# A hybrid transformer block on one Trainium2 core: two late gate blocks as one product of seven, and block sums of the weights added on chip

## The chip, the core and the metric

The kernel runs on one core of one Trainium2 chip. Its engines work side by side, each through its own list of instructions in order, and wait for each other by semaphores. TensorE multiplies matrices: the profile calls it PE, and its weight loads PEld. VectorE (DVE) and ScalarE (ACT) do the elementwise work, GpSimd (POOL) issues transfers that add, and SyncE (SP) issues most other transfers. Matrix products end in PSUM, eight banks of 128 x 512 float32 values; everything else lies in SBUF (on chip) or in DRAM.

The metric is the time of one execution in microseconds (us), less is better. All matrices are float32 in DRAM.

## The reference

One layer with two mixers side by side and a feed-forward part, on 512 tokens of width 1024:

```python
def hybrid_layer(x, ...):
    xn = rmsnorm(x, n_mix_pre)
    proj = xn @ w_in
    qa, ka, va, za, beta_logit, a_dt, qb, kb, vb, gb, gate_a, gate_b = _split_cols(proj, IN_SIZES)
    qkv = jax.nn.silu(causal_depthwise_conv(jnp.concatenate([qa, ka, va], axis=-1), conv_a))
    ...
    oa = chunk_gated_delta_rule(qa, ka, va, beta, g)
    oa = rmsnorm(oa, norm_a) * jax.nn.silu(za.reshape(b, s, A_HEADS, A_DV))
    ya = oa.reshape(b, s, A_V) @ w_br_a
    ...
    ob = chunk_retention(qb, kb, vb)
    ob = rmsnorm(ob, norm_b.reshape(B_HEADS, B_DV)) * jax.nn.silu(gb.reshape(b, s, B_HEADS, B_DV))
    yb = ob.reshape(b, s, B_V) @ w_br_b
    mix = (jax.nn.sigmoid(gate_a) * ya + jax.nn.sigmoid(gate_b) * yb) @ w_out
    x = x + rmsnorm(mix, n_mix_post)
    hn = rmsnorm(x, n_mlp_pre)
    ff = jnp.square(jax.nn.relu(hn @ w_up)) @ w_down
    return x + rmsnorm(ff, n_mlp_post)
```

The columns of `w_in` that matter here: `za` (2048 columns, four blocks of 512, the gates of the delta rule), `vb` and `gb` (2048 each, values and gates of the retention, four heads of 512), `gate_a` and `gate_b` (1024 each).

## The kernel before

**Products in three passes.** To keep float32 accuracy, each operand is split into a high part and a remainder (`split_weights`, L138): ScalarE casts the raw weight tile to `whi` (L145), VectorE subtracts to get `wlo` (L146). Each product is three matmuls, high x high, high x low, low x high. A raw weight tile is 128 x 1024, 512 KB, loaded by the SP queue (L102 or L185). `whi` and `wlo` have three buffers each, the raw tiles two, and four once a second pool (`ych`) has been appended in the second phase.

**Seven products for eight.** Where 512 tokens meet 1024 columns, the product is cut into 2 x 2 x 2 blocks of 256 tokens, 512 rows of the weight and 512 columns. `seven` (L233) computes it with seven block products (Winograd's form of Strassen's method) where eight would be needed. For that it takes sums of blocks of x, made once on chip (`feature_sums`, L1265, called after the second recurrence), and sums of blocks of the weight (`BlockSums`, L152). A block product is two half products (ks = 0 and 1), each of one weight tile and 12 matmuls; its results, two tiles of 128 tokens x 512 columns, lie in a pair of PSUM banks. The products are named by their block of x: "11", "12", "22" and the sums "s1" to "s4". `out(th, ch, ...)` takes a finished block of the output, token half th and column half ch.

**The trickle.** The weight sums are made in DRAM. The SP queue copies a block (`copy_block`, L165), and the GpSimd queue adds another block to it by a transfer that adds (`add_block`, L132). Each unit has four sums, 8 copies and 8 adds of 512 KB. `pace` (L112) issues them behind the weight loads, as far as a budget of model time allows; `JOBS_FROM` is the model time from which it starts.

**Phase one, the delta rule.** The order of TensorE's work is written out by a planner (`Clock`, L618) that keeps a model time, with chains (the inverse, four recurrences, the gating) and fillers, products that it puts between their steps. The fillers stand in a list, each with the events that it needs:

```python
                (ya_filler(1), ("og1",)),
                (value_filler(3), ("og1",)),
                (query_filler(3), ("og1",)),
                (gate_filler(2), ("gate1",)),
                (ya_filler(2), ("og2",)),
                (gate_filler(3), ("gate2",)),
```

`gate_filler(g2)` (L1147) multiplies all tokens by one column block of `za` (4 token tiles x 8 k tiles x 3 passes) and puts Silu of it into `zz`, which has one buffer; the event `gate1` says that the gating of group 1 has used it. On the chip, the third gate group ran from about 312 to 341 us, the fourth from 435 to 467. `recurrence(g2)` (L1157) has four steps; a step multiplies by `kf`, `rt` (L1184), `kd` (L1194) and `dall` (L1213), with small VectorE and ScalarE work between. `gate_chain` (L1233) then gates, transposes and splits the result into `og` (L1258). Matmuls of the planner are pinned to their order; those of the second phase that follow, such as the query and key projections of `scores` (L1384), are not and are put in by a scheduler where it sees room.

**Phase two.** `ya_partial(3)` (L882), then the unit of `gate_a`, four heads each with scores, a value-and-gate unit (`values_and_gates`, L1355) and outputs, then the unit of `gate_b` (`gate_unit`, L1459; `gate_b`, L1504), the final loop (L1521 on) and `w_out`. Inside a unit, the matmuls are pinned to the order of the program (L281). `tc.high_priority(n)` lets an instruction go ahead of others that stand up to n later in the program.

## Time and profile before

| | us |
|---|---|
| median of 3 runs | 1349.88 |
| lowest and highest of them | 1347.24, 1351.58 |
| the profiled execution | 1347.26 |
| its span, first to last instruction | 1345.1 |
| TensorE busy in it | 1327.4 |
| VectorE busy in it | 884.8 |

Times inside the execution count from the start of the span. Matmuls overlap in the pipeline, so the mean duration of one (about 390 ns) is longer than the time from one start to the next; the price of a matmul is read from the chain of waits, which gives the time by which each piece moves the end. Names of tiles stand as output<-inputs, and for a matmul the moving operand comes first: `mm<-whi,actT` streams a weight tile against tokens, `mm<-actT,whi` streams tokens against a weight.

### The profile page before, as it was taken

Reading aid. Unit: us, or ns where it says so; the run is one execution under the profiler, and the core shown is the slowest. Engines: PE = TensorE matmul, PEld = TensorE weight load, DVE = VectorE, ACT = ScalarE, POOL = GpSimd, SP = SyncE. Lnnn points to the kernel's source line nnn. Section 1 sums busy time; section 2 is a strip of 40 time slices with the busy share of each in tenths; the row PEclk is TensorE's granted clock in tenths of the full one; section 3 lists DMA queues with packets and bytes.
Section 4 is the critical chain, followed back from the end, with each engine's and each line's share of the span. In section 5 each row is a group of like instructions: output and inputs, shape, how many; then the busy total and the mean of one; then the engine's idle time right before and its main releaser. Section 6 shows DMA issues by size and latency. Waiting matters only on the chain.

```text
span 1345.1 us, 17540 instructions
## 1 busy us (share of the span) xinstructions
PE 1327.4 (99%) x6639; PEld 1101.2 (82%) x6639; DVE 884.8 (66%) x1515; ACT 634.4 (47%) x1118; POOL 90.9 (7%) x99
## 2 busy tenths in 40 slices
PE   9999999999999999999999999999999999999997
PEld 7888778888888877888888888888889888888886
DVE  6889867475476357777467576679684745828535
ACT  5783426553343424553443443455265746346441
POOL 2201110011101010001001000000100000000000
PEclk9999999999999999999999999999999999999999
DMA  6339987489779685899499695565814543535421
GB/s 193 128 95 244 230 191 149 101 227 207 170 187 210 166 227 161 262 309 221 139 278 194 172 258 142 166 206 173 265 67 147 162 146 110 188 98 179 131 78 63
DMA packets 114691, 236.78 MB, mean 176 GB/s; under 512 B 7398, under 2 KB 31120, under 8 KB 114096
## 3 DMA queue, kind: packets, MB, share of 16 engines
q1 hardware_dynamic: 95792, 185.10, 43.6%
q0 software_dynamic: 16496, 43.69, 19.8%
q10 hardware_dynamic: 2320, 6.89, 1.4%
q8 instruction: 52, 0.85, 0.3%
q14 instruction: 31, 0.25, 0.1%
HBM read 231.43 MB, written 79.71 MB: 231 GB/s over the span
## 4 chain that ended last, share of the span: by engine, by line
PE 86%; DVE 6%; ACT 4%; DMA 3%; issue 1%; DVEq 0%; ACTq 0%
PE mm L627 16%; PE mm L276 13%; PE dl L276 12%; PE mm L92 11%; PE mm L93 11%; PE mm L94 11%; PE dl L627 6%; DMA raw<-in_w_in_dram 2%; DVE wlo L146 1%; PE tr L356 1%; PE dl L93 1%; PE dl L94 1%; PE dl L92 1%; PE tr L636 1%; PE mm L591 1%
## 5 line engine op out<-in xcount | busy, mean ns | idle before, releaser
L146 DVE TENSOR_TENSOR wlo<-raw,whi 128x1024 fp32r<-128x1024 f32 x253 | 309.0, 1224 | 243.8 <-ACT whi L145 243.2
L145 ACT CAST whi<-raw 128x1024 fp32r<-128x1024 f32 x253 | 265.9, 1052 | 403.0 <-PE mm L93 100.1
L627 PE MATMUL mm<-actT,whi 128*128 128x512 f32 x448 | 144.3, 403 | 0.0
L276 PE MATMUL mm<-whi,xsum 128*128 128x512 f32 x384 | 121.9, 390 | 0.0
L94 PE MATMUL mm<-hn,wlo 128*128 128x512 f32 (+1 forms) x288 | 105.4, 366 | 0.0
L93 PE MATMUL mm<-hn,whi 128*128 128x512 f32 (+1 forms) x288 | 105.3, 366 | 0.0
L92 PE MATMUL mm<-hn,whi 128*128 128x512 f32 (+1 forms) x288 | 105.3, 366 | 0.0
L627 PEld LDWEIGHTS mm<-actT,whi 128*128 128x128 f32 x448 | 80.6, 188 | 15.1
L276 PE MATMUL dl<-whi,actT 128*128 128x512 f32 x288 | 91.9, 389 | 0.0
L627 PE MATMUL mm<-whi,actT 128*128 128x512 f32 x256 | 87.8, 406 | 1.1 <-DVE qf L857 1.0
L627 PE MATMUL mm<-actT,wlo 128*128 128x512 f32 x224 | 87.8, 392 | 0.0
L276 PEld LDWEIGHTS mm<-whi,xsum 128*128 128x128 f32 x384 | 72.0, 188 | 14.7
L276 PE MATMUL mm<-wlo,xsum 128*128 128x512 f32 x192 | 74.8, 390 | 0.0
L627 PE MATMUL mm<-whi,og 128*128 128x512 f32 x192 | 64.3, 402 | 0.0
L276 PEld LDWEIGHTS dl<-whi,actT 128*128 128x128 f32 x288 | 54.1, 188 | 11.2
L94 PEld LDWEIGHTS mm<-hn,wlo 128*128 128x128 f32 x288 | 54.3, 189 | 8.8
L93 PEld LDWEIGHTS mm<-hn,whi 128*128 128x128 f32 x288 | 54.3, 189 | 8.7
L92 PEld LDWEIGHTS mm<-hn,whi 128*128 128x128 f32 x288 | 54.3, 189 | 8.7
L276 PE MATMUL dl<-whi,ffq 128*128 128x512 f32 x192 | 61.1, 389 | 0.0
L132 POOL DMA_DIRECT2D sums<-sums x36 | 29.9, 830 | 443.2 <-DMA sums<-in_w_in_dram 238.7
L627 PEld LDWEIGHTS mm<-whi,actT 128*128 128x128 f32 x256 | 48.1, 188 | 11.5 <-issue 1.7
L276 PE MATMUL dl<-wlo,actT 128*128 128x512 f32 x144 | 56.0, 389 | 0.0
(372 smaller groups left out, 2789.7 us busy)
## 6 DMA issues: line engine op xcount, KB each, us to landing
raw<-in_w_in_dram SPq DMA_DIRECT2D x97, 512.0 KB, 5.5
raw<-sums SPq DMA_DIRECT2D x72, 512.0 KB, 4.1
sums<-in_w_in_dram SPq DMA_DIRECT2D x48, 512.0 KB, 8.0
sums<-sums POOLq DMA_DIRECT2D x36, 512.0 KB, 7.9
raw<-in_w_up_dram SPq DMA_DIRECT2D x36, 512.0 KB, 4.2
raw<-in_w_down_dram SPq DMA_DIRECT2D x26, 512.0 KB, 3.8
sums<-in_w_in_dram POOLq DMA_DIRECT2D x24, 512.0 KB, 10.8
sums<-in_w_down_dram SPq DMA_DIRECT2D x24, 512.0 KB, 6.9
```

The costliest lines, as they stand in the source:

```text
L92: nc.tensor.matmul(ps, lh, rh, start=first, stop=False)
L93: nc.tensor.matmul(ps, lh, rl, start=False, stop=False)
L94: nc.tensor.matmul(ps, ll, rh, start=False, stop=last)
L132: tc.keep_in_program_order(nc.gpsimd.dma_start(dst, src, accum_op=ALU.add))
L145: nc.scalar.copy(hi[:, :n], raw[:, :n])
L146: nc.vector.tensor_tensor(lo[:, :n], raw[:, :n], hi[:, :n], ALU.subtract)
L276: m = nc.tensor.matmul(pss[t], lhs[i // 2], rhs[i % 2], start=first and k + i == 0, stop=k + i == 5, skip_group_check=not first,)
L356: nc.tensor.transpose(ps, src, ident)
L591: pin(nc.tensor.matmul(first_keys[f][:, 256:512], ws[w][:, kk, :], xs[x][:, 2 * j + kk, 256:512], start=False, stop=kk == 1 and i == 2, sk ...
L627: m = tc.keep_in_program_order(nc.tensor.matmul(*args, **kwargs))
L636: tc.keep_in_program_order(nc.tensor.transpose(ps, src, ident if by is None else by))
```

## The change

Four things change, and some smaller ones.

The gates of groups 2 and 3 become one filler, `late_gates_filler`, a product of seven over the two column blocks. It stands in the list where the third gate group stood and needs `gate1`; the fourth place is gone. `z_sums` holds its four weight sums, the first in the trickle. The results of group 3 lie in two tiles of their own (`Rows2`), for which `kd` keeps three of four chunks for each head.

The six units of phase two keep two of their four weight sums in DRAM (`full=False`). The other two are made on chip: the raw tile y of sum 3 gets the raw tile x of block 11 added in place after both have been split, and the raw tile of block 21 then gets y added. The order of products becomes 11, s3, s2, 12, 22, s1, s4.

`JOBS_FROM` goes from 60 to 150, and an add may be issued once all copies of its unit have been.

In the last unit the gating of token tiles 0 and 1 moves from `gate_b` into the final loop.

```diff
-JOBS_FROM, LOAD_US, COPY_US, ADD_US, BACKLOG = 60.0, 2.0, 2.0, 3.4, 6.0
+JOBS_FROM, LOAD_US, COPY_US, ADD_US, BACKLOG = 150.0, 2.0, 2.0, 3.4, 6.0
...
+            self.made = (2, 1, 3, 0) if full else (2, 0)
...
+        def raw(self, i, ks):
             while any(job[0] is self for job in trickle):
                 copy_block()
-            while any(dst is t for dst, src in later_adds for t in self.parts):
+            while any(dst is t for dst, *_ in later_adds for t in self.parts):
                 add_block()
-            return block_weights(self.t[i - 1][:, 2 * ks : 2 * ks + 2, :])
+            return block_raw(self.t[i - 1][:, 2 * ks : 2 * ks + 2, :])
...
+    z_sums = BlockSums(w_in, OFF_ZA + 1024, OFF_ZA + 1536, "z")
+    ga_sums = BlockSums(w_in, OFF_GA, OFF_GA + 512, "ga", False)
+    vg_sums = [BlockSums(w_in, OFF_VB + h * 512, OFF_GB + h * 512, f"vg{h}", False) for h in range(4)]
+    gb_sums = BlockSums(w_in, OFF_GBR, OFF_GBR + 512, "gb", False)
...
+        def plus(dst, raws):
+            with tc.high_priority(SUM_PRIO):
+                for d, r in zip(dst, raws):
+                    nc.vector.tensor_tensor(d, r, d, ALU.add)
...
+        x, y = raws(sums.first_raw, 1), raws(sums.raw, 3)
         a = bank(psx)
-        plain(a, "11", 0, c1, True)
+        times(a, "11", x, True)
         with tc.high_priority(400):
             for t in range(2):
                 nc.scalar.copy(p1[t], a[t])
         b = bank(psm)
-        summed(b, "s2", 2, True)
+        times(b, "s3", y, True)
+        plus(y, x)
         with tc.high_priority(400):
             for t in range(2):
-                nc.vector.tensor_tensor(u2[t], p1[t], b[t], ALU.add)
+                nc.vector.tensor_tensor(u3[t], p1[t], b[t], ALU.add)
+        x = raws(sums.first_raw, 3)
         c = bank(psm)
+        times(c, "s2", y, True)
         with tc.high_priority(400):
             for t in range(2):
+                nc.vector.tensor_tensor(p1[t], p1[t], c[t], ALU.add)
+                nc.vector.tensor_tensor(u3[t], u3[t], c[t], ALU.add)
+        times(a, "12", x, False)
+        out(0, 0, a)
+        plus(x, y)
+        d = bank(psm)
+        times(d, "22", x, True)
+        out(1, 0, d, u3, ALU.add)
+        c = bank(psm)
+        times(c, "s1", raws(sums.raw, 1), True)
+        out(1, 1, c, u3, ALU.subtract)
+        times(c, "s4", raws(sums.first_raw, 2), False)
+        out(0, 1, c, p1, ALU.subtract)
...
+        def late_gates_filler():
+            z2 = zzs[2] = pa2.tile([P, 4, T], F32, tag="zz", name="zz")
+            parts = pa2.tile([P, 2, T], F32, name="zz3"), pa2.tile([P, 2, T], F32, tag="qf", name="zz3", bufs=3)
+            zzs[3] = Rows2(parts)
...
+            yield from product(a, "11", None, True)
...
+            yield from product(b, "s2", 2, True)
...
+            yield from product(a, "12", None, False)
+            silu(0, 0, a)
+            yield from product(b, "s3", 3, False)
...
+            yield from product(c, "s1", 1, True)
...
+            yield from product(d, "22", 4, True)
...
+            clock.done("z2", 2.0)
+            yield from product(c, "s4", None, False, OFF_ZA + 1536)
...
+            clock.done("z3", 2.0)
...
-                (gate_filler(2), ("gate1",)),
+                (late_gates_filler, ("gate1",)),
                 (ya_filler(2), ("og2",)),
-                (gate_filler(3), ("gate2",)),
...
-                        nc.vector.tensor_tensor(u[t], ps[t], u[t], op)
-                        out1(row, u[t])
+                        v = tmp("v_s")
+                        nc.vector.tensor_tensor(v, ps[t], u[t], op)
+                        out1(row, v)
...
-                nc.vector.tensor_tensor(sc[:, :n2], ps[:, n - n2 : n], dec[:, :n2], ALU.mult)
+                with tc.high_priority(400):
+                    nc.vector.tensor_tensor(sc[:, :n2], ps[:, n - n2 : n], dec[:, :n2], ALU.mult)
...
             nc.scalar.activation(tb, src, AF.Tanh, scale=0.5)
+            if t < 2:
+                return
...
-                    nc.vector.scalar_tensor_tensor(m, m, 1.0, pss[i][half], ALU.add, ALU.mult)
-                    nc.vector.tensor_tensor(m, m, acc_rows(t, half), ALU.add)
+                    total = pss[i][half]
+                    if t < 2:
+                        rest, total = ya[t // 2][:, t % 2, hs], acc_rows(t, half)
+                        nc.vector.tensor_tensor(total, total, pss[i][half], ALU.add)
+                    else:
+                        rest = acc_rows(t, half)
+                    nc.vector.scalar_tensor_tensor(m, m, 1.0, total, ALU.add, ALU.mult)
+                    nc.vector.tensor_tensor(m, m, rest, ALU.add)
```

## The prediction

> **What bounds the kernel now.** I read the page first: busy times, granted clock, the chain that ended last.

> ```profile
> span 1345.1 us, 17540 instructions
> ...
> PE 1327.4 (99%) x6639; PEld 1101.2 (82%) x6639; DVE 884.8 (66%) x1515; ACT 634.4 (47%) x1118; POOL 90.9 (7%) x99
> ...
> PEclk9999999999999999999999999999999999999999
> ...
> PE 86%; DVE 6%; ACT 4%; DMA 3%; issue 1%; DVEq 0%; ACTq 0%
> ```

> TensorE is busy for 1327.4 of 1345.1 us at full clock and is 86% of the chain. The time is the number of its matmuls plus the few places where it waits. Second, the matmul engine's waits over the whole run, the three longest:

> ```profile
> PE tr L636 <- DVE og L1258: 1.5, 2, 1.2
> PE dl L93 <- DVE wlo L146: 1.4, 1, 1.4
> ...
> PE dl L627 <- DVE rn L1021: 1.0, 1, 1.0
> ```

> No wait is long: what can be won is matmuls, and what can be lost is a new wait in an order that is now almost gapless. Third, the chain of waits inside the second value-and-gate unit (start, length, what):

> ```profile
> 656.49 5.44 PE dl L276 x24
> 661.93 5.44 PE mm L276 x24
> ...
> 672.81 10.88 PE mm L276 x48
> 683.69 5.44 PE dl L276 x24
> 689.13 5.44 PE mm L276 x24
> ```

> Seven products of 24 matmuls follow each other without a gap. One 128x512 matmul costs 5.44 / 24 = 0.227 us of TensorE's time; this is the price of the change's main term. Fourth, busy time by stretch (PE, PEld, DVE, ACT, POOL, clock, DMA share, GB/s): the third gate group, the query and key projections after the delta rule, the first gate unit, the value-and-gate unit above, the last gate unit.

> ```profile
> 312.30:340.60 28.30, 28.26 (x133) 23.40 (x132) 12.31 (x16) 10.78 (x19) 3.19 (x4) 1.00 0.90 193
> ...
> 467.40:496.00 28.60, 28.14 (x131) 22.38 (x130) 15.77 (x36) 10.42 (x23) 2.85 (x3) 1.00 0.73 163
> ...
> 523.90:562.20 38.30, 38.30 (x171) 31.72 (x170) 26.17 (x33) 18.90 (x24) 1.13 (x1) 1.00 0.72 212
> 656.50:694.60 38.10, 38.10 (x169) 31.55 (x169) 24.61 (x27) 19.58 (x23) 1.97 (x2) 1.00 0.81 239
> 889.60:930.10 40.50, 40.43 (x185) 32.69 (x185) 33.40 (x50) 22.66 (x30) 0.00 (x0) 1.00 0.64 202
> ```

> VectorE has 12 to 14 us free in the units, 7 in the last one.

> **Part 1, the late gates.** Column blocks 2 and 3 were two products of 4 token tiles x 8 k tiles x 3 passes, 192 matmuls. Seven products of 2 x 4 x 3 make 168. Removed: 24 x 0.227 = 5.44 us, all on TensorE's path. Added beside it: ten 128x512 VectorE additions and two ScalarE copies, with two weight splits fewer (14 for 16); VectorE is busy 12.3 of 28.3 us there, so they are hidden. The block sums of x are needed some 5 us after 312 instead of 529; the last of them starts at 288.1:

> ```profile
> L212 DVE TENSOR_TENSOR xsum<-full,xsum x4: 1219/1220/1221, 280.2 to 288.1; 128x1024 fp32r<-128x1024 f32 x4
> ```

> The weight sums of the late gates go first in the trickle: 8 copies and 8 adds. In the last 126 us before they are needed the old kernel already landed 12 copies and 14 adds:

> ```profile
> sums<-in_w_in_dram SPq DMA_DIRECT2D x12, 512.0 KB, 6.2
> ...
> sums<-sums POOLq DMA_DIRECT2D x7, 512.0 KB, 8.0
> sums<-in_w_in_dram POOLq DMA_DIRECT2D x7, 512.0 KB, 10.7
> ```

> So they are there in time; cost zero, hidden by the fillers ahead of them. Later units drop 24 copies and 24 adds, so 16 of each fewer in all, on the SP and POOL queues.

> **Part 2, the trickle starts later (60 to 150).** Its first copy left at 95.98, so it moves to about 186. In the stretch that it leaves, one weight load took 13.6 us, against 5.5 in the median, and the chain runs through it:

> ```profile
> 95.98 0.67 SPq L165 DMA_DIRECT2D sums<-in_w_in_dram  x1
> ```
> ```profile
> raw<-in_w_in_dram SPq DMA_DIRECT2D x97, 512.0 KB, 5.5
> ```
> ```profile
> 126.50 13.62 DMA raw<-in_w_in_dram
> ...
> 140.22 1.06 ACT whi L145
> ...
> 141.31 1.22 DVE wlo L146
> ...
> 142.93 2.24 DVE rn L1021
> ```
> ```profile
> 143.87 0.39 PE L627 MATMUL mm<-actT,wlo 128*128 128x512 f32 x1
> 145.31 1.07 PE L627 MATMUL dl<-rn,acc 32*32 32x32 f32 x32 [1.05 <-DVE rn L1021]
> ```

> VectorE works in order: behind the late split stands the end of the inverse, and TensorE stands 145.31 - 143.87 - 0.23 = 1.2 us for it. A load of the median length lets the split start some 2 us earlier, and the wait goes: -1.2 us (bounds: 0, if VectorE's order alone is late, to -1.2).

> **Part 3, the six second-phase units.** Each makes two sums in place, four VectorE additions of 128x1024. The nearest row is the same operation on SBUF tiles:

> ```profile
> L204 DVE TENSOR_TENSOR full<-actT x4: 1217/1218/1221, 226.3 to 273.0; 128x1024 f32<-128x1024 f32 x4
> ```

> 4 x 1.22 = 4.9 us, and two more 128x512 additions out of PSUM at 0.64 (the row at 683.24 below): 6.2 us. VectorE goes to 32.4 of 38.3 and 30.8 of 38.1 us; in the last unit eight operations of about that size leave it (5.1 us), so 34.5 of 40.5, and four return in the final loop. The whi ring has three buffers, so each split has two half products, 5.4 us, of lead; an addition of 1.2 us fits. Four raw buffers now hold x and y through two products, but a buffer is free again four half products (10.9 us) before its next tile is needed, against a load of 5.5. Throughput: zero.

> The order of products is new: "s4" accumulates onto bank pair c directly after "s1", while the subtraction out(1,1) must first read c. Before, "22" (5.44 us) lay between that read and "s4". The orders of matmuls are written out by hand, so everything behind waits with it. Price from the same kind of read behind product "s3":

> ```profile
> 682.10 1.23 DVE L146 TENSOR_TENSOR wlo<-raw,whi 128x1024 fp32r<-128x1024 f32 x1 [1.49 <-ACT whi L145]
> 683.24 1.28 DVE L254 TENSOR_TENSOR p<-p,mm 128x512 f32<-128x512 f32 x2
> ```

> The first read ends at about 683.24 + 0.64 = 683.88; the next product starts at 683.69. In the new order it would start 0.2 us late, with the signal 0.3. The second read has a further 1.36 us and is in time. Bounds for one unit: 0 (the split is issued behind the read) to 1.5 (one more split of 1.2 ahead of it). I take 0.3, since the splits fall in step with the half products: 6 x 0.3 = +1.8 us, bounds 0 and 9.

> [...]

> **Part 4, the tail of the delta rule.** Both late gates now run before the last recurrence. It began at 433.0 and ended at 472.8, with 96 matmuls of the last gate between its steps and the 96 of the next projections behind:

> ```profile
> 433.04 1.02 PE L627 MATMUL dl<-vt,rt 128*128 128x256 f32 x4
> ...
> 472.77 0.66 PE L627 MATMUL dl<-vn,dall 128*128 128x256 f32 x2
> ```
> ```profile
> L627 PE MATMUL mm<-whi,actT 128*128 128x512 f32 x64 | 22.1, 409 | 0.0
> L93 PE MATMUL mm<-actT,whi 128*128 128x512 f32 x32 | 13.3, 415 | 0.0
> ```
> ```profile
> 487.98 0.75 DVE L1258 SCALAR_TENSOR_TENSOR og<-tr,vecs,og 128x512 fp32r<-128x512 f32 x1 [1.47 <-ACT og L1256]
> 490.27 0.75 DVE L1258 SCALAR_TENSOR_TENSOR og<-tr,vecs,og 128x512 fp32r<-128x512 f32 x1 [1.54 <-ACT og L1256]
> ```

> All that stood between the late gates and it moves back by 72 matmuls, 16.3 us: it starts at 449.4. Its cover is the projections, 3 x 32 matmuls = 21.8 us, which are not pinned and can fall between its steps. Its own work is 39.7 - 96 x 0.227 = 17.9 us at most. A step with little filler took

> ```profile
> 216.42 1.03 PE L627 MATMUL dl<-vt,rt 128*128 128x256 f32 x4
> ...
> 222.14 1.13 PE L627 MATMUL dl<-vt,rt 128*128 128x256 f32 x4
> ```

> 5.7 us, so four take about 23. Projections done at 496.0 - 5.4 = 490.6; the gated features come 490.3 + 0.75 - 472.8 = 18 us after the recurrence, and two of the four, enough for the first 12 matmuls, 4.6 us earlier. 449.4 + R + 13.6 <= 490.6 gives R <= 27.6 us; at 23 nothing is lost. I take +0.6 for two or three short waits (bounds 0 and 12.1, R as long as before).

> **Sum**, against the profiled execution (1347.26 us, 2.2 around its span): -5.4 - 1.2 + 1.8 + 0.6 = -4.2, 1343.1. That execution was 2.6 below the median of the runs, 1349.88; on the median: **1345.7 us**, 0.31% less. This measurement can tell about 0.3%, 4 us, from no change: the forecast lies on that bound.

> **Rivals.** *No new waits*: the reads come ahead of the splits, and the 1.4 us wait at L93 for a late split goes with the lighter DMA. -5.4 - 1.2 - 1.4 = -8.0: 1341.9. For it: the free VectorE time above. Against: the split that ends just ahead of the read at 683.24. *The reads queue behind one more split or a value's rounding*: 1.4 per unit, 6 x 1.4 = 8.4; -5.4 - 1.2 + 8.4 + 0.6 = +2.4: 1352.3. At half of that price, -1.8: 1348.1. For it: the value units' out() has no priority of its own; against: the idle 1.49 us in front of each split. *The last recurrence stretches*, the one that ends slower: the list order puts projections between all its steps, R stays at the old 39.7, the gated features are 12.1 us late and nothing else is ready: -5.4 - 1.2 + 1.8 + 12.1 = +7.3: 1357.2. It costs time from R = 27.6 and makes the kernel slower than before from about R = 32.4. For it: R was 39.7 with 96 matmuls as cover; against: the 5.7 us step. *The early wait is VectorE's own*: +1.2, 1346.9, within the forecast's range.

> [...]

> **How the numbers follow.** Forecast (own range 1343.5 to 1348) 0.55, of which 0.30 falls under the bound of -4 us; no new waits 0.17, all faster; queued reads 0.16, a quarter slower; stretched recurrence 0.12, of which 0.10 slower. Faster 0.47, same 0.39, slower 0.14. The range 1341 to 1354 leaves out the stretched end and half of the best case's spread, about 0.2.

> **What would show it.** 24 fewer 128x512 matmuls in phase one; no wait for L1021; loads of the median length between 95 and 185; at the start of each s4 product a TensorE wait of 0.2 to 0.4 us for the subtraction, and none at the other products; the last recurrence starting near 448 and shorter than 28 us, with projections between its steps. Wrong would be waits over 1 us at s4, a gap before the fourth branch product, or waits for sums that have not landed.

## The result, and the profile after

The changed kernel took 1346.11 us in the median of 15 runs (1342.22 to 1349.96), the kernel before 1350.01 in 15 runs beside it (1346.46 to 1352.98). The ratio is 0.9965, with a 95% interval of 0.9953 to 0.9978. The forecast was 1345.7.

First the page and the waits of TensorE over the whole run, as they were read before (waits: us in total, times, longest):

```profile
span 1345.5 us, 17468 instructions
...
PE 1324.8 (98%) x6615; PEld 1096.7 (82%) x6615; DVE 930.4 (69%) x1563; ACT 638.3 (47%) x1126; POOL 78.3 (6%) x83
...
PE 83%; DVE 7%; ACT 4%; DMA 4%; issue 1%; DVEq 0%; ACTq 0%
```
```profile
PE tr L663 <- DVE og L1364: 2.7, 1, 2.7
PE dl L654 <- ACT vt L1314: 2.6, 1, 2.6
...
PE mm L303 <- DVE u L1574: 0.4, 1, 0.4
```

The records hold 24 matmuls fewer, and neither the wait for L1021 nor the one at L93 is there. Two waits of 2.6 and 2.7 us are new or longer, and the DMA's share of the chain rose from 3% to 4%. The span did not shrink with the median: the profiled execution took 1347.26 us, as that of before did. It is one of the slower of its 15 runs, that of before one of the faster of its own. A ledger of the stages shows where the gains go in these executions (time of the first or last matmul of a stage by the timeline; "again" is a second profiled execution of the changed kernel):

| | before | changed | again |
|---|---|---|---|
| first step of the first recurrence | 190.7 | 189.1 | 190.1 |
| first matmul of the late gates (before: of the third gate group) | 312.3 | 312.2 | 312.6 |
| first matmul of the first gate unit | 523.9 | 520.8 | 520.8 |
| last matmul of head 0's outputs | 606.7 | 604.5 | 604.4 |
| last matmul of head 3's outputs | 889.4 | 888.1 | 888.0 |
| last branch product of the final loop | 955.2 | 955.6 | 955.1 |
| last matmul | 1337.2 | 1337.6 | 1337.0 |

Phase one wins 3.1 us where the forecast had 6.0 (5.4 + 1.2 - 0.6), and wins none of it before the late gates begin (312.2 and 312.6 against 312.3). Then 0.9 is lost up to the outputs of head 0, 0.9 up to those of head 3, and 1.3 to 1.8 in the last unit and the final loop.

The chain of waits inside the late gates shows what was lost there (start, length, what):

```profile
334.02 1.05 ACT whi L145
335.10 1.24 DVE wlo L146
336.35 7.29 DMA raw<-sums
343.72 1.06 ACT whi L145
344.80 1.24 DVE wlo L146
346.05 6.73 DMA raw<-in_w_in_dram
...
352.89 1.04 ACT whi L145
353.93 0.75 ACT vt L1314 x2
...
354.72 2.63 PE dl L654 x8
```

In the kernel before, TensorE alone stood on the chain here. Now a loop stands on it: cast, subtract, and only then the load of the tile that takes the same buffer. There are two raw buffers, so one turn (9.7 us from 334.02 to 343.72) serves two tiles, 24 matmuls, 5.44 us of TensorE's work. A raw tile of the old gates served 24 matmuls by itself; one of a block product serves 12. When the cast at 352.89 comes late, the scaling of the recurrence (L1314) stands behind it on ScalarE, and TensorE waits 2.6 us for that. Behind this wait the clock is halved for 3.41 us, which costs 1.7 more (last section).

### The profile page after: what moved, and what is told of

The parts are those of the page before. It is cut to its first block, busy times and chain, and to the rows that moved or that the text cites. A ratio compares the mean times of both kernels' runs of the same rounds, so it can differ in the third digit from the quotient of the medians.

```text
span 1345.5 us, 17468 instructions
## 1 busy us (share of the span) xinstructions
PE 1324.8 (98%) x6615; PEld 1096.7 (82%) x6615; DVE 930.4 (69%) x1563; ACT 638.3 (47%) x1126; POOL 78.3 (6%) x83
## 3 DMA queue, kind: packets, MB, share of 16 engines
q1 hardware_dynamic: 88592, 167.27, 39.7%
## 4 chain that ended last, share of the span: by engine, by line
PE 83%; DVE 7%; ACT 4%; DMA 4%; issue 1%; DVEq 0%; ACTq 0%
PE mm L654 15%; PE mm L303 14%; PE mm L93 11%; PE mm L92 11%; PE mm L94 11%; PE dl L303 9%; PE dl L654 5%; DVE wlo L146 2%; DMA raw<-in_w_in_dram 2%; DMA raw<-sums 2%; PE dl L94 1%; PE dl L92 1%; PE dl L93 1%; PE tr L383 1%; PE tr L663 1%
## 5 line engine op out<-in xcount | busy, mean ns | idle before, releaser
L145 ACT CAST whi<-raw 128x1024 fp32r<-128x1024 f32 x259 | 272.1, 1052 | 415.3 <-PE mm L93 104.1
L146 DVE TENSOR_TENSOR wlo<-raw,whi 128x1024 fp32r<-128x1024 f32 x259 | 316.0, 1223 | 216.3 <-ACT whi L145 215.1
L654 PE MATMUL mm<-actT,whi 128*128 128x512 f32 x448 | 144.3, 403 | 0.0
L93 PE MATMUL mm<-hn,whi 128*128 128x512 f32 (+1 forms) x288 | 105.3, 366 | 0.0
L654 PE MATMUL mm<-actT,wlo 128*128 128x512 f32 x224 | 87.7, 392 | 0.0
L654 PE MATMUL mm<-whi,actT 128*128 128x512 f32 x176 | 61.3, 410 | 1.0 <-DVE qf L892 1.0
L93 PEld LDWEIGHTS mm<-hn,whi 128*128 128x128 f32 x288 | 54.3, 189 | 8.7
L303 PE MATMUL dl<-whi,actT 128*128 128x512 f32 x192 | 61.1, 389 | 0.0
L1771 DVE TENSOR_TENSOR ffq<-r,ffq 128x512 fp32r<-128x512 f32 (+2 forms) x51 | 33.8, 678 | 29.1 <-ACT ffq L1771 29.0
L92 PE MATMUL mm<-actT,whi 128*128 128x512 f32 x128 | 51.5, 403 | 0.0
L132 POOL DMA_DIRECT2D sums<-in_w_in_dram x28 | 32.6, 1167 | 321.3 <-DMA sums<-in_w_in_dram 321.0
L94 PE MATMUL mm<-actT,wlo 128*128 128x512 f32 x128 | 50.8, 397 | 0.0
## 6 DMA issues: line engine op xcount, KB each, us to landing
raw<-in_w_in_dram SPq DMA_DIRECT2D x95, 512.0 KB, 4.8
raw<-sums SPq DMA_DIRECT2D x56, 512.0 KB, 4.0
raw<-in_w_up_dram SPq DMA_DIRECT2D x36, 512.0 KB, 3.9
sums<-in_w_in_dram SPq DMA_DIRECT2D x32, 512.0 KB, 7.4
sums<-in_w_in_dram POOLq DMA_DIRECT2D x28, 512.0 KB, 8.1
raw<-in_w_down_dram SPq DMA_DIRECT2D x26, 512.0 KB, 3.8
sums<-in_w_down_dram SPq DMA_DIRECT2D x24, 512.0 KB, 12.5
sums<-sums POOLq DMA_DIRECT2D x16, 512.0 KB, 8.3
```

Source lines behind the costliest of these rows:

```text
L92: nc.tensor.matmul(ps, lh, rh, start=first, stop=False)
L93: nc.tensor.matmul(ps, lh, rl, start=False, stop=False)
L94: nc.tensor.matmul(ps, ll, rh, start=False, stop=last)
L132: tc.keep_in_program_order(nc.gpsimd.dma_start(dst, src, accum_op=ALU.add))
L145: nc.scalar.copy(hi[:, :n], raw[:, :n])
L146: nc.vector.tensor_tensor(lo[:, :n], raw[:, :n], hi[:, :n], ALU.subtract)
```

## The experiments

All ratios are to the kernel before, run beside each on the same chip.

**The change again**, unaltered.

> The changed kernel once more, unaltered, for a second profiled execution beside the first. Theory (late weights): each raw tile of the late gates serves 12 matmuls, 2.72 us, and with two raw buffers a tile takes half of a load and its split, (5.4 + 1.1 + 1.2) / 2 = 3.9 us, so TensorE waits there in every execution: 5 to 8 us lost between 300 and 375, in other places than the first time, and a median of 1346 +- 1. Rival (an accident of the one execution): under 3 us lost there, with no TensorE wait above 1.5 us in the late gates, and the same median.

1343.97 us (12 runs, 1342.19 to 1348.13; before 1350.74), ratio 0.9957 [0.9944, 0.9970]. Its profiled execution, of 1346.76 us, has the two waits at the same places; TensorE's waits:

```profile
PE dl L654 <- ACT vt L1314: 2.4, 1, 2.4
PE tr L663 <- DVE og L1364: 2.0, 1, 2.0
```

Late weights are no accident of one execution. The median of 1346 +- 1 that went with this theory was missed: it is 1 us lower.

**Two raw buffers more in the late gates.** The tile that later holds the values of group 3 takes every second weight tile.

```diff
+            def late(block):
+                if 3 not in vts and clock.events.get("og1", float("inf")) <= clock.now:
+                    vts[3] = pa2.tile([P, 4, 4, P], F32, tag="vt", name="vt", bufs=2)
+                n = next(seen) if 3 in vts else 0
+                if n % 2 == 0:
+                    return block_raw(block)
+                raw = vts[3].rearrange("p a c n -> p (a c n)")[:, 1024 * (n // 2 % 2) :][:, :1024]
```

> The changed kernel with two more raw buffers for the late gates, from the time on at which the first delta values are transposed: the tile that later takes the values of group 3 holds every second weight tile of the late gates. Theory (late weights, two buffers too few): a tile then takes 7.7 / 4 = 1.9 us, less than its 2.72 us of matmuls; the waits between 325 and 370 go, -3 to -5.5: 1341 to 1343, ratio 0.993 to 0.995. Rival (the DMA is full: 0.81 busy there): the loads only start earlier and take longer, -1 or less, ratio 0.996. Rival (VectorE's and ScalarE's order: splits ahead of the recurrence's scaling): the waits for the scaling stay or grow, 1346 or more.

1343.94 us (6 runs, 1341.86 to 1345.45), ratio 0.9960 [0.9945, 0.9976]. TensorE's waits between 303 and 375:

```profile
PE tr L663 <- DVE og L1379: 2.2, 1, 2.2
PE mm L654 <- DVE wlo L146: 0.8, 1, 0.8
PE mm L654 <- ACT whi L145: 0.5, 1, 0.5
```

The wait for the scaling is gone, and from 320.83 on the chain is TensorE's alone again, although each load took longer (median 7.7 to 9.4 us against 5.4 to 5.9). The first gate unit starts at 517.5, 6.4 earlier than before the change; the changed kernel won 3.1. The other traces say the same: the first gate unit starts at 517.3 to 518.5 in the three kernels with the two more buffers, and at 519.7 to 525.2 in the eight executions of kernels that have the late gates without them. So the mechanism is shown in profiled executions, where its price here is 3.3 us. The median did not follow: 1343.94 against 1343.97, which is what the rival of the full DMA expected. How large the loss is in the other runs stays open.

**Product s4 in a bank pair of its own**, with two VectorE operations more.

```diff
-        times(c, "s4", raws(sums.first_raw, 2), False)
-        out(0, 1, c, p1, ALU.subtract)
+        with tc.high_priority(400):
+            for t in range(2):
+                nc.vector.tensor_tensor(p1[t], c[t], p1[t], ALU.subtract)
+        e = bank(psx)
+        times(e, "s4", raws(sums.first_raw, 2), True)
+        out(0, 1, e, p1, ALU.add)
```

> The changed kernel, but product s4 of each of the six units starts in a bank pair of its own; the difference c - p1 is taken while it runs and s4 is added to it, two more 128x512 VectorE operations per unit. Theory (the read of s1 ahead of s4 costs 0.3 in a value unit, 0.9 in the first gate unit, up to 2 in the last): the waits for L1574 and its like at s4 go, -1.5 to -3 against the changed kernel: 1341 to 1343, ratio 0.993 to 0.9945. Rival (the two operations more only move the wait to the next product or the transposes): within 0.5 of the changed kernel, ratio 0.9955 to 0.997, with waits at the start of the scores or the last transposes in place of those at s4.

1342.84 us (6 runs, 1342.31 to 1344.76), ratio 0.9950 [0.9931, 0.9970]. The stretches by the ledger:

| us | before | changed | s4 in own banks |
|---|---|---|---|
| first gate unit to outputs of head 0 | 82.8 | 83.7 | 82.8 |
| from there to outputs of head 3 | 282.7 | 283.6 | 282.8 |
| from there to the last branch product | 65.8 | 67.6 (again 67.1) | 66.6 |

The first gate unit and the value units have their old length again, so the read of s1 ahead of s4 is their whole cost: 0.9 in the first row, which holds the value unit of head 0 too, and 3 x 0.3 in the second. In the last unit the read explains 0.5 to 1.0, and 0.8 is left. The medians do not tell this kernel from the changed one.

**22 between s1 and s4**, the order of products 11, s3, s2, 12, s1, 22, s4.

```diff
-        d = bank(psm)
-        times(d, "22", x, True)
-        out(1, 0, d, u3, ALU.add)
         c = bank(psm)
         times(c, "s1", raws(sums.raw, 1), True)
         out(1, 1, c, u3, ALU.subtract)
+        d = bank(psm)
+        times(d, "22", x, True)
+        out(1, 0, d, u3, ALU.add)
```

> The changed kernel with the order 11, s3, s2, 12, s1, 22, s4 in the six units: 5.44 us of product 22 lie again between the read of s1 and s4, with no operation more. Theory (the read costs): the same -1.5 to -3 as with banks of their own, ratio 0.993 to 0.9945. Rival (raw buffers): the summed tile of 22 is held through s1, so a load for s4 starts one product, 5.4 us, later; a load takes 4.4 to 4.9 us and its split 2.3, so TensorE waits for wlo at s4, 0.5 to 2 per unit: +1 to +9, ratio 0.997 to 1.003.

1354.65 us (12 runs), ratio 1.0035 [1.0021, 1.0050]: slower, in the direction of the rival. TensorE's waits between 525 and 800:

```profile
PE tr L383 <- DVE og L369: 3.0, 2, 1.8
PE mm L303 <- DVE wlo L146: 1.5, 2, 0.8
```

It waits for wlo as the rival said, but loses more where transposes wait for the split of the gated features, which neither side named. The order is not the only difference: an add of the trickle is issued at 548.8 in the first gate unit, where the changed kernel issues none between 528.4 and 570.9.

**The trickle from 60 again**, the rest as changed.

```diff
-JOBS_FROM, LOAD_US, COPY_US, ADD_US, BACKLOG = 150.0, 2.0, 2.0, 3.4, 6.0
+JOBS_FROM, LOAD_US, COPY_US, ADD_US, BACKLOG = 60.0, 2.0, 2.0, 3.4, 6.0
```

> The changed kernel with the trickle from 60 again. Theory (the forecast): the wait of 1.2 us for L1021 near 145 comes back, +1.2, 1345 to 1347, ratio 0.9965 to 0.9975. Rival (the trickle's adds cost where they fall on loads with little lead): adds that are done 90 us earlier leave the units freer, the late gates too: -1 to -4, ratio 0.993 to 0.995.

1357.56 us (6 runs, 1354.11 to 1360.44), ratio 1.0058 [1.0037, 1.0080]. Both expectations missed: by the ratios (1.0058 against 0.9965 and 0.9957) the early start costs 12.6 to 13.6 us, not 1.2. TensorE's waits:

```profile
PE mm L303 <- DVE u L1574: 7.1, 1, 7.1
...
PE dl L654 <- DVE rn L1056: 1.9, 1, 1.9
```

The wait of the forecast is back (the second line, the old L1021), and a far larger one stands in the first gate unit. The timeline there (start, busy, what, idle before and its releaser):

```profile
556.54 1.04 ACT L145 CAST whi<-raw 128x1024 fp32r<-128x1024 f32 x1 [4.34 <-DMA raw<-in_w_in_dram]
...
557.62 1.23 DVE L146 TENSOR_TENSOR wlo<-raw,whi 128x1024 fp32r<-128x1024 f32 x1 [4.01 <-ACT whi L145]
...
558.76 1.28 DVE L1574 TENSOR_TENSOR u<-mm,u 128x512 f32<-128x512 f32 x2
...
559.59 0.76 PE L303 MATMUL mm<-whi,xsum 128*128 128x512 f32 x1 [7.05 <-DVE u L1574]
```

A load is late, its split stands ahead of the read of s1 on VectorE, and s4 waits for the read: the forecast's rival of reads that queue behind a split, made worse by a late load. The loads and adds issued between 535 and 556, here and then in the changed kernel (KB each, median us to landing):

```profile
raw<-in_w_in_dram SPq DMA_DIRECT2D x4, 512.0 KB, 13.7
...
sums<-sums POOLq DMA_DIRECT2D x1, 512.0 KB, 8.3
sums<-in_w_down_dram POOLq DMA_DIRECT2D x1, 512.0 KB, 15.2
```
```profile
raw<-in_w_in_dram SPq DMA_DIRECT2D x4, 512.0 KB, 5.5
```

With two adds of the trickle beside them the same loads take 13.7 us; with none, 5.5.

**The trickle from 60 and s4 in its own banks**, the two edits above together.

> The changed kernel with the trickle from 60 and with product s4 in a bank pair of its own. Theory (the early trickle costs 10 us because its adds fall on the weight loads of the first gate unit, the last split is late, and the read of s1 stands behind it on VectorE, with s4 behind the read): without the read only the lateness of the split is left; the 7.1 us at 552 shrink to 1 or 2, the waits before the outputs stay away, and the 1.2 at L1021 remains: 1344 to 1348, ratio 0.996 to 0.999. Rival (the loads themselves are 7 us late, whatever waits for the read): 1352 or more, with waits for wlo in the first gate unit in place of L1574.

1353.79 us (12 runs), ratio 1.0035 [1.0018, 1.0051]. The wait of 7.1 us is gone; what is left of waits from 530 to 610 is small, the longest 0.9 us, though the loads still took 12.7 us. The largest in total:

```profile
PE dl L307 <- DVE wlo L146: 1.2, 2, 0.8
```

From the first gate unit's start to the outputs of head 0 it takes 87.7 us, against 94.1 with s4 in the old banks and 82.8 before the change, so the read did multiply the lateness there. But 1344 to 1348 was expected, and the median is 6 us above. In this execution TensorE also waits 3.3 us for the recurrence's scaling in the late gates, and the first gate unit starts at 525.2, 4.4 later than in the changed kernel. That part does not come with the early trickle in every execution: with the old banks the first gate unit started at 519.7, earlier than in the changed kernel.

**The late gates alone**: the six units as before, with four sums each in DRAM; the trickle from 150.

```diff
-    ga_sums = BlockSums(w_in, OFF_GA, OFF_GA + 512, "ga", False)
+    ga_sums = BlockSums(w_in, OFF_GA, OFF_GA + 512, "ga")
...
-        x, y = raws(sums.first_raw, 1), raws(sums.raw, 3)
+        plain, summed = block_products(src, sums, product)
```

> The late gates as a product of seven and the trickle from 150, with the six units, their four sums in DRAM and the last gating as before the change. Theory (late weights): -5.4 for 24 matmuls, -1.2 for the early wait, -1.4 for the wait at 510, +5 to +6.5 of new waits in the late gates: -1.5 to -3, 1347 to 1348.5, a ratio of 0.998 to 0.999. Rival (the forecast's sum: the late gates cost nothing at the side): -5.4 - 1.2 + 0.6 = -6.0, 1344, a ratio of 0.9955.

1360.32 us (6 runs, 1352.68 to 1365.12), ratio 1.0082 [1.0055, 1.0109]. Both missed. The profiled execution is the lowest of the six, 7.6 below their median, so it shows only a part of the loss. Up to the first gate unit it won 2.6, in the first unit of the down projection it lost 5.7, where adds and copies still ran (issues from 1040 to 1092, KB each, median us to landing; no copy and no add is issued there in the changed kernel):

```profile
raw<-in_w_up_dram SPq DMA_DIRECT2D x5, 512.0 KB, 12.7
...
sums<-in_w_down_dram SPq DMA_DIRECT2D x4, 512.0 KB, 11.8
sums<-in_w_down_dram POOLq DMA_DIRECT2D x4, 512.0 KB, 16.5
```

**The same with the trickle from 60.**

> The late gates as a product of seven, with the six units as before (four sums each in DRAM) and the trickle from 60. Theory (the trickle is too late: with 16 jobs more than before and a start at 150, the sums of the down projection are still being added when its first unit runs, which lost 5.8 us there): with the start at 60 this loss goes: 1345 to 1349, ratio 0.996 to 0.999. Rival (the volume: more adds beside the loads wherever they fall): 1353 or more, ratio 1.002 or more.

1353.46 us (12 runs), ratio 1.0033 [1.0013, 1.0052]. The start at 60 takes the loss in the down projection from 5.7 to some 1 us, as the theory said, but the time stays in the rival's range. Its execution loses 3.7 in the late gates at the state of the recurrence (the line below), and reaches the first gate unit at 524.1, no earlier than before the change; 4.0 more go up to the outputs of head 0. In this execution the volume costs as well, in other places.

```profile
PE dl L637 <- DVE st L1287: 3.7, 1, 3.7
```

**The units alone**: the gates of groups 2 and 3 as two products of all tokens.

```diff
-                (late_gates_filler, ("gate1",)),
+                (gate_filler(2), ("gate1",)),
                 (ya_filler(2), ("og2",)),
+                (gate_filler(3), ("gate2",)),
```

> The six units with two sums added in place, the trickle from 150 and the last gating as in the changed kernel; the gates of groups 2 and 3 are two products of all tokens again. Theory (late weights): the units cost 1.1 in the middle and 2.0 at the end, -1.2 to -1.6 early, -1.4 at 510: +0 to +1, 1350 to 1351, a ratio of 1.000 to 1.001. Rival (the units are the gain, the late gates give all of theirs back): -2 or more, ratio 0.9985 or less. Rival (the forecast's sum): -1.2 + 1.8 = +0.6, the same time as the theory; the waits at s4 then stand at 0.3 each.

1353.48 us (7 runs), ratio 1.0039 [1.0022, 1.0057]; every expectation was lower. Most of the loss is again in one place, TensorE's longest wait, with 1.7 us at a halved clock behind it:

```profile
PE mm L302 <- DVE u L1574: 3.3, 1, 3.3
```

With eight copies and adds fewer ahead of them, two adds of the down sums reach the first gate unit, and its four loads take 9.9 us.

**The kernel before with the trickle from 150.**

```diff
-JOBS_FROM, LOAD_US, COPY_US, ADD_US, BACKLOG = 60.0, 2.0, 2.0, 3.4, 6.0
+JOBS_FROM, LOAD_US, COPY_US, ADD_US, BACKLOG = 150.0, 2.0, 2.0, 3.4, 6.0
```

> The kernel before, with the trickle from 150 in place of 60 and nothing else. Theory (a late start pays only where the volume has shrunk): the wait for L1021 goes, -1.2, but 72 copies and adds start 90 us later, so that more of them fall on the units and on the first down projection: +2 to +8, 1352 to 1358, ratio 1.0015 to 1.006. Rival (the forecast's step by itself): -1.2 and no other difference, ratio 0.998 to 1.0.

1351.61 us (12 runs), ratio 1.0018 [1.0004, 1.0033]. The wait for L1021 is gone, and the kernel is slower by 0.2%, at the lower end of the theory: this step alone is no gain.

**Both additions**: two raw buffers more and s4 in its own banks.

> The changed kernel with both: two raw buffers more for the late gates, and s4 in banks of its own. Theory (late weights in the late gates cost 3 us, the reads 2): both add up against the changed kernel, 1340 to 1341.5, ratio 0.992 to 0.9935, below each of the two alone. Rival (what is won in the late gates is lost again before the units, as the medians of the two extra buffers alone said): as with s4 alone, 1342.5 to 1344, ratio 0.994 to 0.9955.

1341.65 us (6 runs, 1339.85 to 1342.86), ratio 0.9944 [0.9921, 0.9966]. It is faster than the kernel before, and has the lowest ratio measured here. In time it lies just above the theory's range, by the ratio in the rival's. Its interval overlaps that of the changed kernel, so how much it gains on that one is not settled; its last matmul is at 1333.1, that of the changed kernel at 1337.0 and 1337.6.

**Both additions, the last unit with its old order and four sums in DRAM.**

```diff
-    gb_sums = BlockSums(w_in, OFF_GBR, OFF_GBR + 512, "gb", False)
+    gb_sums = BlockSums(w_in, OFF_GBR, OFF_GBR + 512, "gb")
...
-        gate_unit(gb_sums, OFF_GBR, gate_b)
+        gate_unit(gb_sums, OFF_GBR, gate_b, seven_old, 1)
```

> Both additions (two raw buffers more, s4 in banks of its own), and in the last unit alone the old order of products with all four sums made in DRAM, 4 copies and 4 adds more in the trickle. Theory (the in-place additions overload VectorE in the last unit, where it was busiest): the waits of 0.4 to 0.6 at the transposes of o and in the final loop go, -1 to -1.5 against both additions alone. Rival (the last unit's waits come from the scaling and the transposes, not from the additions): no gain, 0 to +1.

1352.36 us (12 runs), ratio 1.0020 [1.0003, 1.0036]. The last unit does win what was expected: from the end of head 3's outputs to the last branch product 65.5 us against 66.7, with less VectorE work (columns as in the prediction's stretches; first this kernel, then both additions alone):

```profile
892.00:957.50 65.50, 65.43 (x310) 53.27 (x308) 54.44 (x80) 30.57 (x41) 4.15 (x5) 1.00 0.65 190
```
```profile
884.10:950.80 66.70, 65.55 (x305) 52.96 (x304) 59.10 (x87) 30.14 (x40) 1.70 (x3) 1.00 0.56 171
```

But four copies and four adds more in the trickle move its adds: the loads issued between 575 and 600 take 10.4 us against 5.6, and the outputs of head 0 wait 4.0 us. From the start of the first gate unit to the end of those outputs it takes 89.3 us, against 82.8 with both additions alone:

```profile
PE dl L92 <- DVE gs L1514: 4.0, 1, 4.0
```

## Why the prediction was right, and where it was not

The number held, 1346.11 against 1345.7. Its sum did not, step by step; as far as the traces tell, the number was met by luck.

**Part 1.** The 24 matmuls went. The step that failed is "so they are hidden", and with it the count "two weight splits fewer (14 for 16)". A raw tile holds two k tiles of 512 columns, so the two old products took 8 loads and 8 splits, and the product of seven takes 14 of each: six more, not two fewer. The records have them (VectorE's splits over the whole run, before and after):

```profile
L146 DVE TENSOR_TENSOR wlo<-raw,whi x253: 1195/1225/1233, 29.4 to 1278.4; 128x1024 fp32r<-128x1024 f32 x127
```
```profile
L146 DVE TENSOR_TENSOR wlo<-raw,whi x259: 1195/1225/1230, 29.4 to 1278.8; 128x1024 fp32r<-128x1024 f32 x130
```

The forecast looked at VectorE's free time and at the sums, and not at how fast two raw buffers turn when a tile serves 12 matmuls. From the first matmul of the late gates to the first gate unit the changed kernel won 3.0 and 3.4 us. About 2.0 of that the sum did not hold: TensorE's waits between 380 and 524, 2.4 us before (the 1.4 at L93 among them), are 0.3 and 0.4 after. So the term -5.4 was worth about -1 in the profiled executions. With two more buffers this stretch won 6.6, so the term was worth about -4.5.

**Part 2.** The wait for L1021 went, and comes back, at 1.9 us, with the old start. The loads issued from 95 to 185, before and after (KB each, median us to landing):

```profile
raw<-in_w_in_dram SPq DMA_DIRECT2D x12, 512.0 KB, 7.9
```
```profile
raw<-in_w_in_dram SPq DMA_DIRECT2D x12, 512.0 KB, 3.7
```

But the wait moved on. Near 303 TensorE waits for the gated features that it transposes (`og`), and the load ahead of them on the chain takes longer (before; changed; the kernel before with the trickle from 150):

```profile
287.78 7.22 DMA raw<-in_w_in_dram
```
```profile
286.18 9.64 DMA raw<-in_w_in_dram
```
```profile
289.06 11.20 DMA raw<-in_w_in_dram
```

This wait is 0.8 to 1.2 us in the four kernels whose trickle starts at 60, and 1.6 to 3.3 in the ten traces with a start at 150. So the late gates began no earlier than the third gate group had (312.2 and 312.6 against 312.3), and the term -1.2 was worth about nothing. The step also priced only what the trickle left. Where it went decides far more: going back to 60 costs 12.6 to 13.6 us in the changed kernel, while going to 150 costs 2.8 in the kernel before (0.5 to 4.5 by its interval). The same holds for the 16 copies and 16 adds saved, to which the forecast gave no price: four of each more (both additions with the old last unit) or eight fewer (the units alone) moved the adds onto other loads.

**Part 3.** The wait at s4 is there, 0.38 us in the first gate unit:

```profile
553.18 1.28 DVE L1574 TENSOR_TENSOR u<-mm,u 128x512 f32<-128x512 f32 x2
...
554.01 0.47 PE L303 MATMUL mm<-whi,xsum 128*128 128x512 f32 x1 [0.38 <-DVE u L1574]
```

It costs 0.3 in each of the value units of heads 1 to 3, as taken. The first gate unit and head 0 cost 0.9 together and the last unit 1.3 to 1.8, so the term is +3.1 to +3.5 and not +1.8. That VectorE's additions cost nothing held in five units. In the last, which was named as the tightest, 0.8 is left; it is gone (65.5 us) in the kernel with both additions where this unit has its old order and four sums in DRAM and keeps the moved gating, so it belongs to the new order with its additions in place and not to the gating.

**Part 4** held: the last recurrence ran from 453.85 to 474.2, 20 us, with projections between its steps (its start in the timeline, its end in the chain), and the one wait behind it, at its transposes, is 0.3 us. It started 4.4 us later than the 449.4 of the forecast, which fits the loss in the late gates (3.1 us of waits and 1.7 at the halved clock).

```profile
453.85 1.02 PE L654 MATMUL dl<-vt,rt 128*128 128x256 f32 x4
```
```profile
473.72 0.52 PE dl L654 x2
```

**The sum.** In the profiled executions the change is worth between +0.4 and -0.2 us at the last matmul, not -4.2: about 3 us counted as won in phase one were not (of 5.4 + 1.2 - 0.6 = 6.0 about 1 came from the matmuls, and 2 from waits that the sum did not hold), and some 1.5 were missing in the units. Against the medians it is -3.9, and -6.8 in the second comparison. The forecast moved its sum from the profiled execution to the median by 2.6, which was right for the kernel before; the profiled executions of the changed kernel lie 1.2 and 2.8 above their medians. So the two misses cancel. Executions of one kernel spread over 6 to 11 us where there are 12 or more. The longer ones have the lower mean clock (the kernel before: 0.999 at 1346.22 us, 0.992 at 1354.77), which fits more stalls of the kind in the last section; where they lie in an execution without a trace stays open, and with it where the typical execution of the changed kernel wins its 4 us.

**The rivals.** The reads behind one more split did not decide here, but did in two of the partial kernels (3.3 and 7.1 us). The stretched recurrence did not occur. Of *no new waits* one part came true: the 1.4 us at L93 went, beside new waits elsewhere.

What the forecast did not have at all: the parts are no sum. Late gates alone are 0.8% slower than before, units alone 0.4%, a late trickle alone 0.2%, all but the late start 0.6%; together they are 0.35% faster. In the traces of the first two and the last, adds of the trickle fall beside loads with little lead; in the whole none is issued beside the loads for s1 and s4 of the first gate unit, nor in the first down projection.

## What to carry to other kernels

When a product is cut so that a weight tile serves fewer matmuls, count its loads and splits again, and compare the tile's matmul time with (load + split) / buffers (here 2.72 us against 9.7 / 2 = 4.9), before counting the saved matmuls. A wait that goes early is worth only what is left of it behind the next wait (here nothing: the late gates began at 312.2 and 312.6, against 312.3). Background transfers cost by where they land (here loads of 5.5 us took 13.7 with two adds beside them), so a change in their number or start is a change to every load beside them, and its parts can't be judged one by one. A read that an accumulating product has to await inherits the delays of what stands ahead of it in its engine's order (here the wait at s4 was 0.38 us, and 7.1 where a late split stood ahead of the read).

## What the runs showed that was not expected

A 512 KB load of the first gate unit that took 4.9 to 5.5 us with no adding transfer issued beside it took 8.4 to 13.7 in the four kernels with two of them (medians of four loads each).

```profile
352.53:355.94 3.41, 1.22 (x6) 1.09 (x7) 1.24 (x2) 3.05 (x7) 0.00 (x0) 1.00 1.04 227
355.94:359.35 3.41, 3.41 (x10) 2.66 (x9) 2.60 (x4) 1.60 (x5) 0.00 (x0) 0.50 0.46 146
...
301.33:304.74 3.41, 1.50 (x9) 1.33 (x10) 3.14 (x6) 1.70 (x4) 0.15 (x1) 1.00 0.69 94
304.74:308.15 3.41, 3.41 (x19) 2.83 (x18) 1.95 (x3) 2.35 (x3) 0.00 (x0) 1.00 0.99 201
```
```profile
350.75:354.16 3.41, 1.83 (x9) 1.18 (x7) 1.19 (x3) 0.37 (x1) 0.34 (x1) 1.00 0.99 284
354.16:357.57 3.41, 1.94 (x9) 1.74 (x10) 1.97 (x3) 3.38 (x10) 0.00 (x0) 1.00 0.75 142
357.57:360.99 3.42, 3.42 (x18) 2.83 (x16) 3.04 (x5) 1.53 (x2) 0.00 (x0) 1.00 0.61 161
```

In the halved step of the changed kernel a 128x512 matmul starts 0.43 us after the one before it, against 0.227 at full clock. TensorE is busy throughout that step and does the work of 1.7 us in it, so 1.7 us belong to the wait. The forecast had left the clock out, as no wait was long.
